# A batched x·yᵀ on Trainium2: five slots of 2 MB become two adjacent pairs and a single, with 4 MB stores and 32 KB reads

## The chip, the cores and the metric

The kernel runs on one NeuronCore of one Trainium2 chip. The metric is the time of one execution on the device in microseconds (us), the median of the runs given. Besides these there is one execution taken by the hardware profiler; its span runs from the first to the last instruction. The engines are called PE (TensorE, matmuls), DVE (VectorE), ACT (ScalarE), POOL (GpSimd) and SP (SyncE, which here does nothing but issue DMAs). Sixteen DMA engines move the data between the main memory and the on-chip memory.

## What is computed

```python
# x: 8 x 12 x 512 x 64 fp32,  y: 8 x 12 x 512 x 64 fp32
np.einsum('bhtc,bhsc->bhts', x, y)      # out: 8 x 12 x 512 x 512 fp32
```

For each of the 96 heads (8 x 12) this is a 512 x 64 matrix times the transpose of another 512 x 64 matrix, and 1 MB of output. Read are 25.17 MB in all, written 100.66 MB.

## The kernel before, in words

**Groups and tiles.** The 96 heads go in 6 groups of 16 (`NG`). A group's x, and its y, is one load of 2 MB into a slot of 128 partitions with 16 KB each: 12 loads, `load(0)` to `load(11)`, x and y in turn. A group has two halves of 8 heads, so there are 12 halves (`NH`). A half gives 8 MB of output in 4 results of 2 MB (`V`), each again 128 partitions with 16 KB. So 48 results `o` are stored, each from one slot.

**Slots.** Five slots of 2 MB (`SLOTS`) serve loads and results alike. `slot()` (L123) gives them out in turn, 0 to 4 and again. A slot's next user waits until the last one has read or stored it; `emit` (L86) keeps for every buffer who wrote and who reads it, and `need` (L71) turns that into waits on semaphores. Each slot has a semaphore of its own for its DMAs.

**From load to product.** `compress(n)` (L136) makes bf16 of a load: for x one ACT copy into `xk`, for y four casts into `yb` (two by DVE, one by POOL, one by ACT). `mix` (L160) rearranges a half's x into `xb` by 32-partition copies, by POOL for the first three halves and by DVE for the rest. `transposes` (L175) turns `xb` and `yb` with DVE into `xT` and `yT`, which are there twice, for halves in turn. `products` (L197) makes 4 matmuls of 128 x 512 into one of the two PSUM buffers `pm`, and a copy (L110; by ACT, and by DVE for the two results in `late`) brings it to half a slot. Two of these make a result.

**Stores.** `store(o, s)` (L211) sends a slot's 2 MB out: 128 reads of 16 KB from the partitions, 128 writes of 16 KB to the output, in an order of 64 x 2 rows. ACT issues every third store and the last four (`by_act`, L208); those wait in `later` until the first copy of the next result is under way (L229). SP issues the others, and all loads.

**The order of the work** is that of the program's lines from L245 on; each engine runs its own instructions in this order. SP first issues five loads. A loop over the 12 loads (L257) then compresses load n and issues load n + 5 for n below 5; load 10 is issued after n = 6 and load 11 after n = 8, into the slots 1 and 3. The four results of the first half come in the same loop: the first after `compress(8)`, the second after `compress(9)`, the third after `compress(10)`, the fourth ahead of `compress(11)`. The other 44 results follow, and after every fourth the transposes and the mixing for a later half (`prepare`, L237).

Of the kernel before, what the change touches and what calls it, by code (L numbers as in the profile page):

```python
# [9 lines left out]
def kernel(  # L10
# [8 lines left out]

    nc = tc.nc
    B, H, T, C = x.shape
    _, _, S, _ = y.shape
    P = 128
    G = 16
    Q = P // G
    R = T // Q
    NG = B * H // G  # L40
    NH = 2 * NG
    V = G // 4
    K = 8
    E = R // K
    D = 32
    SLOTS = 5
    fp32 = mybir.dt.float32
    bf16 = mybir.dt.bfloat16
    u32 = mybir.dt.uint32
    COPY = mybir.ActivationFunctionType.Copy  # L50
    assert C == 2 * D and S == T and R == 2 * D and Q * V == D

    xv = x.rearrange("b h t c -> (b h t c)").rearrange("(g p n) -> g p n", p=P, n=R * C)
    yv = y.rearrange("b h t c -> (b h t c)").rearrange("(g p n) -> g p n", p=P, n=R * C)
    ov = out.rearrange("b h t s -> (b h t s)").rearrange(
        "(o u h q n) -> o h q u n", u=2, h=V, q=Q * E, n=K * S
    )

    sb = ctx.enter_context(tc.tile_pool(name="sb", bufs=1))
    ps = ctx.enter_context(tc.tile_pool(name="ps", bufs=1, space=bass.MemoryType.PSUM))  # L60
    slots = [sb.tile([P, K * S], fp32, name=f"slot{i}") for i in range(SLOTS)]
    xks = [sb.tile([P, R, C], bf16, name=f"xk{i}") for i in range(NG - 1)]
    ybs = [[sb.tile([P, R // 2 * D], u32, name=f"yb{h}{i}") for i in range(NG - 1 + h)] for h in range(2)]
    xbs = [sb.tile([P, K * E * D], u32, name=f"xb{half}") for half in range(2)]
# [2 lines left out]
    pms = [ps.tile([P, 4, S], fp32, name=f"pm{i}") for i in range(2)]  # L67
    engines = {"act": nc.scalar, "dve": nc.vector, "pool": nc.gpsimd, "pe": nc.tensor, "sp": nc.sync}
    sems, ticks, known, snaps, writer, readers = {}, {}, {e: {} for e in engines}, {}, {}, {}

    def need(name, points):  # L71

        best = {}
        for p, v in points:
            if known[name].get(p, 0) < v:
                best[p] = max(best.get(p, 0), v)
        for p, v in list(best.items()):
            if any(snaps[q, w].get(p, 0) >= v for q, w in best.items() if q != p):
                del best[p]
        for p, v in best.items():  # L80
            engines[name].wait_ge(sems[p], v)  # L81
            known[name][p] = v
            for q, w in snaps[p, v].items():
                known[name][q] = max(known[name].get(q, 0), w)

    def emit(name, make, reads=(), writes=(), dma=None):  # L86

        points = [writer[r] for r in (*reads, *writes) if r in writer]
        points += [v for w in writes for v in readers.get(w, ())]
        if name == "pool" and name in ticks:  # L90
            points.append((name, ticks[name]))
        need(name, points)
        p, step = (name, 1) if dma is None else (f"dma{dma}", 16)
        if p not in sems:
            sems[p] = tc.alloc_semaphore(p)
        make().then_inc(sems[p], step)
        at = (p, ticks.get(p, 0) + step)
        ticks[p] = at[1]
        snaps[at] = {**known[name], p: at[1]}
        if dma is None:  # L100
            snaps[at][name] = at[1]
        for r in reads:
            readers.setdefault(r, []).append(at)
        for w in writes:
            writer[w], readers[w] = at, []

    made_slots, loaded, later, late = [], {}, [], (V * NH - V - 1, V * NH - 1)
    in_front = ["dve", "pool", "dve", "act"]

    def copy(name, dst, src, reads, writes):  # L110
        emit(
            name,
            lambda: nc.scalar.activation(dst, src, COPY)  # L113
            if name == "act"
            else engines[name].tensor_copy(dst, src),  # L115
            reads,
            writes,
        )

    def both(i):  # L120
        return [("slot", i, 0), ("slot", i, 1)]

    def slot():  # L123
        made_slots.append(len(made_slots) % SLOTS)
        return made_slots[-1]

    def load(n):
        i = loaded[n] = slot()
        emit(
            "sp",  # L130
            lambda: nc.sync.dma_start(slots[i], (yv if n % 2 else xv)[n // 2]),  # L131
            writes=both(i),
            dma=i,
        )
# [40 lines left out]
    def transposes(i):  # L175
        g, half = divmod(i, 2)
        b = g % (NG - 1 + half)
        emit(
            "dve",
            lambda: nc.vector.transpose(  # L180
                xTs[half].rearrange("p (k r e) -> p k e r", k=K, e=E),
                xbs[half].rearrange("p (k e c) -> p k e c", k=K, e=E),
            ),
            [("xb", half, part) for part in range(4)],
            [("xT", half)],
        )
        emit(
            "dve",
            lambda: nc.vector.transpose(  # L189
                yTs[half].rearrange("p (r j) -> p j r", r=D),  # L190
                ybs[half][b].rearrange("p (j c) -> p j c", c=D),
            ),
            [("yb", half, b, ch) for ch in range(2)],
            [("yT", half)],
        )

    def products(o, k):  # L197
        i, h = divmod(o, V)
        xT = xTs[i % 2].bitcast(bf16).rearrange("p (k h m) -> p k h m", k=K, h=V)
        yT = yTs[i % 2].bitcast(bf16)  # L200
        for j in range(4):
            last = nc.tensor.matmul(  # L202
                pms[k // 4][:, j, :], xT[:, k + j, h, :], yT[:, h * S:(h + 1) * S],
                start=True, stop=True,
            )
        return last

    def by_act(o):  # L208
        return o % 3 == 2 or o >= V * NH - V

    def store(o, s):  # L211
        i, h = divmod(o, V)
        name = "act" if by_act(o) else "sp"
        emit(
            name,
            lambda: engines[name].dma_start(ov[i, h], slots[s]),
            reads=both(s),
            dma=s,
        )

    def result(o, s):

        ot = slots[s].rearrange("p (r s) -> p r s", s=S)
        for k in range(0, K, 4):
            pm = k // 4
            half = o // V % 2
            emit("pe", lambda: products(o, k), [("xT", half), ("yT", half)], [("pm", pm)])
            copy("dve" if o in late else "act", ot[:, k:k + 4, :], pms[pm], [("pm", pm)], [("slot", s, pm)])
            if k == 0:  # L229
                while later:  # L230
                    store(*later.pop())
        if by_act(o):
            later.append((o, s))
        else:
            store(o, s)

    def prepare(i):  # L237

        if i < NH:
            transposes(i)  # L240
        if i + 1 < NH:
            for part in range(4):
                mix(i + 1, "dve", part)

    with tc.tile_critical():  # L245
        load(0)
        for half, name in enumerate(("dve", "pool")):
            emit(
                name,
                lambda: engines[name].memset(xbs[half], 0.0),  # L250
                writes=[("xb", half, part) for part in range(4)],
            )
        need("sp", [("pool", 1)])
        for g in range(1, SLOTS):
            load(g)
        front = []
        for n in range(2 * NG):  # L257
            if n == 11:
                result(3, slot())
            compress(n)  # L260
            mix(n // 4, "pool", n % 4)
            if n == 4:
                transposes(0)
            if n < 5:
                load(n + SLOTS)
            elif n in (6, 8):
                load(n // 2 + 7)
            elif n < 10:
                front.append(slot())
            if n > 7 and n < 11:  # L270
                result(n - 8, front[n - 8])
            if n == 9:
                transposes(1)
        prepare(2)
        for o in range(V, V * NH):
            result(o, slot())
            if o % V == V - 1:
                prepare(o // V + 2)
        store(*later.pop())
        for i, name in enumerate(("dve", "pool", "dve", "pe", "act")):  # L280
            need(name, [(f"dma{i}", ticks[f"dma{i}"])])
# [30 lines left out]
```

## Time and profile before

| what | value |
|---|---|
| median of 3 runs | 300.97 us (300.89 to 301.33) |
| profiled execution, span | 299.1 us (299.07 in the trace) |
| ACT busy | 204.1 us (68%) |
| DVE busy | 160.7 us (54%) |
| PE busy | 129.2 us (43%), mean granted clock 0.796 |
| POOL busy | 56.0 us (19%) |
| SP's DMA queue (q1) | 6048 packets, 88.08 MB, 69.3% of 16 engines |
| ACT's DMA queue (q10) | 2592 packets, 37.75 MB, 29.6% of 16 engines |
| stores, issue to landing | 16.7 us (SP), 14.8 us (ACT), medians |
| copy of half a result by ACT | 1884 ns, 92 of them |

How to read it: the profiled span is 1.9 us shorter than the median of the runs, which also have what lies around it. A busy share is of the whole span. The two queue shares are the time that packets took, summed over the 16 DMA engines and divided by 16 spans. In the tables by line, a group of instructions is given as engine, operation and output tile from input tile; most copies have the line of a helper (L113, L115), so a group is told apart by its tiles. The timeline lists a start, a length, and the instructions that were merged. The chain of waits follows the last instruction back to what released it; in this profile 57% of it is DMA and 22% ACT.

### The profile page before, as it was taken

Reading aid. Unit: us, or ns where it says so; the run is one execution under the profiler, and the core shown is the slowest. Engines: PE = TensorE matmul, PEld = TensorE weight load, DVE = VectorE, ACT = ScalarE, POOL = GpSimd, SP = SyncE. Lnnn points to the kernel's source line nnn. Section 1 sums busy time; section 2 is a strip of 40 time slices with the busy share of each in tenths; the row PEclk is TensorE's granted clock in tenths of the full one; section 3 lists DMA queues with packets and bytes.
Section 4 is the critical chain, followed back from the end, with each engine's and each line's share of the span. In section 5 each row is a group of like instructions: output and inputs, shape, how many; then the busy total and the mean of one; then the engine's idle time right before and its main releaser. Section 6 shows DMA issues by size and latency. Waiting matters only on the chain.

```text
span 299.1 us, 1163 instructions
## 1 busy us (share of the span) xinstructions
PE 129.2 (43%) x377; PEld 35.4 (12%) x384; DVE 160.7 (54%) x77; ACT 204.1 (68%) x105; POOL 56.0 (19%) x23
## 2 busy tenths in 40 slices
PE   0000040547556556474545565554546464567100
PEld 0000010111111111111111111111111111111000
DVE  2167897999839590940946819319276340500500
ACT  1665676999999895687776868685959595549000
POOL 2399999991000000000000000000000000000000
PEclk9999995657799977685979685959795959775655
DMA  7999999999999999999999999999999999999996
GB/s 267 432 427 436 430 425 421 436 432 430 425 438 432 423 436 433 425 430 436 432 423 437 430 421 436 434 427 425 436 430 425 425 427 425 432 425 425 430 425 256
DMA packets 8645, 125.90 MB, mean 421 GB/s; under 512 B 960, under 2 KB 960, under 8 KB 960
## 3 DMA queue, kind: packets, MB, share of 16 engines
q1 hardware_dynamic: 6048, 88.08, 69.3%
q10 hardware_dynamic: 2592, 37.75, 29.6%
q8 instruction: 3, 0.05, 0.1%
q14 instruction: 2, 0.02, 0.0%
HBM read 25.17 MB, written 100.66 MB: 421 GB/s over the span
## 4 chain that ended last, share of the span: by engine, by line
DMA 57%; ACT 22%; PE 6%; issue 5%; DVE 3%; POOL 1%; SPq 0%; ACTq 0%; POOLq 0%
DMA out_dram<-slot 44%; ACT slot L113 19%; DMA slot<-in_y_dram 7%; DMA slot<-in_x_dram 6%; PE pm L202 6%; DVE yb L115 2%; DVE slot L115 2%; ACT xk L113 1%; ACT yb L113 1%; POOL xb L250 1%; SPq L131 0%; ACTq L81 0%; POOLq L307 0%; SPq L245 0%
## 5 line engine op out<-in xcount | busy, mean ns | idle before, releaser
L113 ACT ACTIVATE slot<-pm 128x2048 f32<-128x2048 f32 x92 | 166.6, 1884 | 49.8 <-DMA out_dram<-slot 41.9
L202 PE MATMUL pm<-yT,xT 128*128 128x512 bf16 x377 | 129.2, 482 | 148.3 <-ACT slot L113 108.3
L180 DVE STREAM_TRANSPOSE xT<-xb 128x2048 uint32<-128x2048 uint32 x12 | 46.6, 3887 | 71.3 <-PE pm L202 68.9
L202 PEld LDWEIGHTS pm<-yT,xT 128*128 128x128 bf16 x384 | 35.4, 113 | 241.6 <-ACT slot L113 140.3
L115 DVE COPY xb<-xk 32x2048 bf16<-32x2048 bf16 x36 | 46.9, 1303 | 1.0
L115 DVE CAST yb<-slot 64x2048 bf16<-64x2048 f32 x12 | 36.2, 3013 | 17.0 <-DMA slot<-in_y_dram 16.8
L115 POOL COPY xb<-xk 32x2048 bf16<-32x2048 bf16 x12 | 36.2, 3019 | 10.5 <-ACT xk L113 9.7
L113 ACT ACTIVATE xk<-slot 128x4096 bf16<-128x4096 f32 x6 | 21.7, 3617 | 16.4 <-DMA slot<-in_x_dram 16.4
L115 DVE COPY slot<-pm 128x2048 f32<-128x2048 f32 x4 | 9.0, 2286 | 29.4 <-PE pm L202 29.4
L189 DVE STREAM_TRANSPOSE yT<-yb 128x1024 uint32<-128x1024 uint32 x12 | 23.1, 1921 | 0.0
L113 ACT ACTIVATE yb<-slot 64x2048 bf16<-64x2048 f32 x6 | 14.7, 2457 | 5.1 <-DMA slot<-in_y_dram 5.1
L115 POOL CAST yb<-slot 64x2048 bf16<-64x2048 f32 x6 | 17.8, 2968 | 1.4 <-DMA slot<-in_y_dram 0.8
L250 DVE MEMSET xb<- 128x2048 uint32 x1 | 1.8, 1765 | 1.4 <-SPq L245 1.4
L113 ACT ACT_TABLE_LOAD x1 | 1.3, 1283 | 0.9 <-SPq L245 0.9
L250 POOL MEMSET xb<- 128x2048 uint32 x1 | 1.8, 1804 | 0.5 <-SPq L245 0.5
L296 POOL MEMSET const-float32-0.0<- 128x1 f32 x1 | 0.1, 98 | 0.2 <-issue 0.2
L296 POOL MEMSET const-float32-1.0<- 128x1 f32 x1 | 0.1, 98 | 0.0
L296 POOL MEMSET const-bfloat16-1.0<- 128x1 bf16 x1 | 0.1, 98 | 0.0
L296 POOL MEMSET const-uint8-127<- 128x1 uint8 x1 | 0.1, 98 | 0.0
## 6 DMA issues: line engine op xcount, KB each, us to landing
out_dram<-slot SPq DMA_DIRECT2D x30, 2048.0 KB, 16.7
out_dram<-slot ACTq DMA_DIRECT2D x18, 2048.0 KB, 14.8
slot<-in_x_dram SPq DMA_DIRECT2D x6, 2048.0 KB, 17.3
slot<-in_y_dram SPq DMA_DIRECT2D x6, 2048.0 KB, 20.3
```

What stands on the lines that cost most here:

```text
L113: lambda: nc.scalar.activation(dst, src, COPY)
L115: else engines[name].tensor_copy(dst, src),
L180: lambda: nc.vector.transpose(xTs[half].rearrange("p (k r e) -> p k e r", k=K, e=E), xbs[half].rearrange("p (k e c) -> p k e c", k=K, e=E),),
L189: lambda: nc.vector.transpose(yTs[half].rearrange("p (r j) -> p j r", r=D), ybs[half][b].rearrange("p (j c) -> p j c", c=D),),
L202: last = nc.tensor.matmul(pms[k // 4][:, j, :], xT[:, k + j, h, :], yT[:, h * S:(h + 1) * S], start=True, stop=True,)
L250: lambda: engines[name].memset(xbs[half], 0.0),
L296: nc = _bacc.Bacc("TRN2", target_bir_lowering=False, num_devices=1)
```

## The change

Slots 0 and 1 become one buffer of 128 partitions with 32 KB each, slots 2 and 3 another, and slot 4 stays by itself. They lie at fixed places; the rest of the memory is given out as before.

- **Stores.** Two results in an adjacent pair of slots go out in one DMA of 4 MB: 128 reads of 32 KB, and 256 writes of 16 KB in an order of 64 x 4 rows. Such a pair is made of the results 0 and 2, or 1 and 3, of a half, since these lie at one step in the output. Other results go out by themselves as before. A table (`plan`) says which result goes where: in the first half a pair and two singles, in the second a single, a pair and a single, and then in turn two pairs, or a single, a pair and a single. That makes 17 stores of 4 MB and 14 of 2 MB.
- **Loads.** Loads 2 to 11 read 64 rows of 32 KB and write 128 rows of 16 KB. Loads 0 and 1 stay as they were.
- **How they are issued.** `wide` makes the DMA instruction by hand, with the two sides' access patterns as they are given.
- **Who issues.** SP issues all stores but those of the last half, which ACT issues. DVE makes the copies of one result, the last, instead of two.
- **Order.** Load 10 is issued after `compress(7)` into slot 2, and load 11 after `compress(8)` into slot 3. In the first half the results are made in the order 0, 2, 1, 3; the first store comes after result 2.

```diff
-    slots = [sb.tile([P, K * S], fp32, name=f"slot{i}") for i in range(SLOTS)]
+    xw, yw = (a.rearrange("(g p n) -> g p n", p=P // 2, n=2 * N) for a in (xf, yf))
+    ow = of.rearrange("(o a j q n) -> o j q a n", a=4, j=2, q=Q * E, n=N)
+    pairs = [nc.alloc_sbuf_tensor(f"slots{i}", [P, 2 * N], fp32)[:, :] for i in range(2)]
+    slots = [p[:, j * N:(j + 1) * N] for p in pairs for j in range(2)]
+    slots.append(nc.alloc_sbuf_tensor("slot", [P, N], fp32)[:, :])
...
+    places = [0, 1, 2, 3, 4, 0, 1, 2, 3, 4, 2, 3]
+    steady = [
+        [(0, 2, 0), (1, 3, 2)],
+        [(0, 4), (1, 3, 0), (2, 4)],
+        [(0, 2, 2), (1, 3, 0)],
+        [(0, 4), (1, 3, 2), (2, 4)],
+    ]
+    plan = [[(0, 2, 0), (1, 4), (3, 2)], [(0, 3), (1, 3, 0), (2, 4)]]
+    plan += [steady[i % 4] for i in range(2, NH)]
...
+    def place(ap, dims):
+        name = ap.tensor.name
+        pattern = [ap.ap[0], *[[1, 1]] * (dims - len(ap.ap)), *ap.ap[1:]]
+        return mybir.PhysicalAccessPattern(
+            ap=pattern, offset=ap.offset, dtype=ap.dtype, memref=name, memsetref=f"{name}_set"
+        )
+
+    def wide(name, dst, src):
+        return engines[name].add_instruction(
+            mybir.InstDMACopy(
+                name=nc.get_next_instruction_name(),
+                engine=engines[name].engine,
+                ins=[place(src, len(dst.ap))],
+                outs=[place(dst, len(dst.ap))],
+                mode="Copy",
+                cce_op=mybir.AluOpType.bypass,
+                queue="qActDynamicHW" if name == "act" else "qSPDynamicHW",
+            )
+        )
+
     def load(n):
-        i = loaded[n] = slot()
+        i = loaded[n] = places[n]
         emit(
             "sp",
-            lambda: nc.sync.dma_start(slots[i], (yv if n % 2 else xv)[n // 2]),
+            lambda: nc.sync.dma_start(slots[i], (yv if n % 2 else xv)[n // 2])
+            if n < 2
+            else wide("sp", slots[i], (yw if n % 2 else xw)[n // 2]),
...
-    def store(o, s):
-        i, h = divmod(o, V)
-        name = "act" if by_act(o) else "sp"
+    def store(i, *what):
+        *hs, s = what
+        name = "act" if i == NH - 1 else "sp"
         emit(
             name,
-            lambda: engines[name].dma_start(ov[i, h], slots[s]),
-            reads=both(s),
+            lambda: wide(name, ow[i, hs[0]], pairs[s // 2])
+            if len(hs) == 2
+            else engines[name].dma_start(ov[i, hs[0]], slots[s]),
+            reads=both(*range(s, s + len(hs))),
             dma=s,
         )
...
+    def results(i, *what):
+        *hs, s = what
+        for j, h in enumerate(hs):
+            result(i, h, s + j)
+        if i == NH - 1:
+            later.append((i, *what))
+        else:
+            store(i, *what)
...
             if n < 5:
                 load(n + SLOTS)
-            elif n in (6, 8):
-                load(n // 2 + 7)
-            elif n < 10:
-                front.append(slot())
-            if n > 7 and n < 11:
-                result(n - 8, front[n - 8])
-            if n == 9:
+            elif n in (7, 8):
+                load(n + 3)
+            if n == 8:
+                result(0, 0, 0)
+            elif n == 9:
+                result(0, 2, 1)
+                store(0, *plan[0][0])
                 transposes(1)
+            elif n == 10:
+                results(0, *plan[0][1])
         prepare(2)
-        for o in range(V, V * NH):
-            result(o, slot())
-            if o % V == V - 1:
-                prepare(o // V + 2)
+        for i in range(1, NH):
+            for what in plan[i]:
+                results(i, *what)
+            prepare(i + 2)
         store(*later.pop())
```

More of the change, by code (lines that the diff above doesn't have):

```diff
@@ L46 @@
     SLOTS = 5
+    N = K * S
     fp32 = mybir.dt.float32
@@ L50 @@
     COPY = mybir.ActivationFunctionType.Copy
[L51 to L57, printed above, removed]
+    assert C == 2 * D and S == T and R == 2 * D and Q * V == D and N == R * C
+    xf, yf, of = (a.rearrange("b h t c -> (b h t c)") for a in (x, y, out))
+    xv, yv = (a.rearrange("(g p n) -> g p n", p=P, n=N) for a in (xf, yf))
+    xw, yw = (a.rearrange("(g p n) -> g p n", p=P // 2, n=2 * N) for a in (xf, yf))
+    ov = of.rearrange("(o u h q n) -> o h q u n", u=2, h=V, q=Q * E, n=N)
+    ow = of.rearrange("(o a j q n) -> o j q a n", a=4, j=2, q=Q * E, n=N)
+    pairs = [nc.alloc_sbuf_tensor(f"slots{i}", [P, 2 * N], fp32)[:, :] for i in range(2)]
+    slots = [p[:, j * N:(j + 1) * N] for p in pairs for j in range(2)]
+    slots.append(nc.alloc_sbuf_tensor("slot", [P, N], fp32)[:, :])
     sb = ctx.enter_context(tc.tile_pool(name="sb", bufs=1))
     ps = ctx.enter_context(tc.tile_pool(name="ps", bufs=1, space=bass.MemoryType.PSUM))
-    slots = [sb.tile([P, K * S], fp32, name=f"slot{i}") for i in range(SLOTS)]
     xks = [sb.tile([P, R, C], bf16, name=f"xk{i}") for i in range(NG - 1)]
@@ L105, in emit @@
             writer[w], readers[w] = at, []
-    made_slots, loaded, later, late = [], {}, [], (V * NH - V - 1, V * NH - 1)
+    loaded, later = {}, []
     in_front = ["dve", "pool", "dve", "act"]
+    places = [0, 1, 2, 3, 4, 0, 1, 2, 3, 4, 2, 3]
[7 more added lines that the diff above has]
+    plan += [steady[i % 4] for i in range(2, NH)]
     def copy(name, dst, src, reads, writes):
@@ L118, in copy, with both @@
         )
[L120 to L125, printed above, removed]
+    def both(*ids):
+        return [("slot", i, pm) for i in ids for pm in range(2)]
+    def place(ap, dims):
[16 more added lines that the diff above has]
+        )
     def load(n):
-        i = loaded[n] = slot()
+        i = loaded[n] = places[n]
         emit(
             "sp",
-            lambda: nc.sync.dma_start(slots[i], (yv if n % 2 else xv)[n // 2]),
+            lambda: nc.sync.dma_start(slots[i], (yv if n % 2 else xv)[n // 2])
+            if n < 2
+            else wide("sp", slots[i], (yw if n % 2 else xw)[n // 2]),
             writes=both(i),
@@ L206, in products, with result @@
         return last
-    def by_act(o):
-        return o % 3 == 2 or o >= V * NH - V
-    def store(o, s):
-        i, h = divmod(o, V)
-        name = "act" if by_act(o) else "sp"
+    def store(i, *what):
+        *hs, s = what
+        name = "act" if i == NH - 1 else "sp"
         emit(
             name,
-            lambda: engines[name].dma_start(ov[i, h], slots[s]),
-            reads=both(s),
+            lambda: wide(name, ow[i, hs[0]], pairs[s // 2])
+            if len(hs) == 2
+            else engines[name].dma_start(ov[i, hs[0]], slots[s]),
+            reads=both(*range(s, s + len(hs))),
             dma=s,
         )
-    def result(o, s):
+    def result(i, h, s):
         ot = slots[s].rearrange("p (r s) -> p r s", s=S)
+        late = i == NH - 1 and h == plan[i][-1][-2]
         for k in range(0, K, 4):
             pm = k // 4
-            half = o // V % 2
-            emit("pe", lambda: products(o, k), [("xT", half), ("yT", half)], [("pm", pm)])
-            copy("dve" if o in late else "act", ot[:, k:k + 4, :], pms[pm], [("pm", pm)], [("slot", s, pm)])
+            half = i % 2
+            emit("pe", lambda: products(i * V + h, k), [("xT", half), ("yT", half)], [("pm", pm)])
+            copy("dve" if late else "act", ot[:, k:k + 4, :], pms[pm], [("pm", pm)], [("slot", s, pm)])
             if k == 0:
@@ L231, in result @@
                     store(*later.pop())
-        if by_act(o):
-            later.append((o, s))
+    def results(i, *what):
[4 more added lines that the diff above has]
+            later.append((i, *what))
         else:
-            store(o, s)
+            store(i, *what)
     def prepare(i):
@@ L253 @@
         need("sp", [("pool", 1)])
-        for g in range(1, SLOTS):
-            load(g)
-        front = []
+        for n in range(1, SLOTS):
+            load(n)
         for n in range(2 * NG):
             if n == 11:
-                result(3, slot())
+                results(0, *plan[0][2])
             compress(n)
```

## The prediction

> **What bounds the kernel now.** I read the page from its second part, the span in forty slices, and the packet line under it.
>
> ```profile
> DMA  7999999999999999999999999999999999999996
> GB/s 267 432 427 436 430 425 421 436 432 430 425 438 432 423 436 433 425 430 436 432 423 437 430 421 436 434 427 425 436 430 425 425 427 425 432 425 425 430 425 256
> DMA packets 8645, 125.90 MB, mean 421 GB/s; under 512 B 960, under 2 KB 960, under 8 KB 960
> ```
>
> The 16 DMA engines are full from the second slice to the last but one. The trace's packet records say the same to the nanosecond: from the first packet at 1.99 us to the last data at 297.6 us no engine idles, through loads and stores alike. So the span is 1.99 us of start, 480 packets of 16 KB on each engine, and about 1.5 us of end. Only two things can move it: what a packet takes, and a hole in the stream. Both the load stage and the store stage run at nearly one rate, as the windows by stage show (the last two columns are the DMA's busy share and GB/s):
>
> ```profile
> 10.00:30.00 20.00, 0.00 (x0) 0.00 (x0) 11.21 (x4) 12.55 (x5) 17.06 (x6) 1.00 1.00 429
> 60.00:100.00 40.00, 22.93 (x74) 6.35 (x73) 31.37 (x16) 39.50 (x22) 8.40 (x3) 0.83 1.01 431
> 200.00:290.00 90.00, 43.39 (x128) 11.84 (x128) 36.12 (x18) 53.48 (x30) 0.00 (x0) 0.77 1.01 428
> ```
>
> ACT (the fourth engine in these rows) is busy 39.50 of 40 us between 60 and 100 us. There ACT is as full as the DMA, so what it makes later, the DMA gets later. The timelines of ACT, DVE and SP around the first stores are what the holes are worked out from:
>
> ```profile
> 57.60 3.65 ACT L113 ACTIVATE slot<-pm 128x2048 f32<-128x2048 f32 x2
> 61.27 3.62 ACT L113 ACTIVATE xk<-slot 128x4096 bf16<-128x4096 f32 x1
> 64.80 3.63 ACT L113 ACTIVATE slot<-pm 128x2048 f32<-128x2048 f32 x2
> ...
> 83.97 10.73 ACT L113 ACTIVATE slot<-pm 128x2048 f32<-128x2048 f32 x6
> ```
> ```profile
> 36.75 13.71 DVE L115 CAST yb<-slot 64x2048 bf16<-64x2048 f32 x4
> ```
> ```profile
> 41.80 0.33 SPq L131 DMA_DIRECT2D slot<-in_x_dram  x1
> 51.59 0.33 SPq L131 DMA_DIRECT2D slot<-in_y_dram  x1
> 55.12 6.69 SPq L216 DMA_DIRECT2D out_dram<-slot  x2
> ```
>
> Here the first result is stored at 55.12 and the second at 61.27, while by the packet records the twelfth load keeps the engines until 61.53 (first engine) to 62.13 (last). The early store at 55.12 is the cover that the change takes away.
>
> **Part 1: the packets.** In the records of 10 to 30 us a 16 KB packet starts every 607 ns on its engine, and a transfer's 4-byte closing packet takes 6 ns: 8 x 607 + 6 = 4862 ns per 2 MB, seen again and again. Two rows price a packet apart from its data: the 4-byte packet's 6 ns, and two undisturbed 8 KB records of 309 ns beside 611 ns for 16 KB (2 x 309 - 611 = 7). I take 5 ns a packet, so about 602 ns of data. The change makes 32 KB reads; writes stay 16 KB, so the trace of before can't say whether the 5 ns belong to a read or to a write. Bounds: nothing (they belong to the write) and 7 ns per read saved. Below nothing: a read could lose by being paired with two writes; the nearest row is that loads of 128 rows and stores of 64 x 2 rows both run at 4862 ns, so unequal sides have cost nothing here, and I leave 2 ns for it. I take 5, the nearest row to a bare packet. [...]
>
> There are 17 pair stores and 14 single ones in place of 48. A pair saves 8 reads x 5 + one closing packet of 6 = 46 ns per engine. A wide load saves 4 x 5 = 20 ns: loads 2 to 8 together 0.14 us, which is how much sooner load 8 lands. ACT runs without slack from that landing (47.95) on, so all its times below move up by 0.14.
>
> **Part 2: the holes in front.** (a) Load 10 now goes into slot 2, which DVE's casts of load 7 read; they end at 36.75 + 13.71 = 50.46, where before the issue stood at 41.80. Load 11 behind it on SP waits for ACT anyway until 51.56. How long from an issue to the first packet with an empty queue? One row: the first load, issued at 0.96, first packet at 1.99, 1.03 us, of which 0.39 is the issue. Store issues take 0.54 to 0.65, so I take 1.2 us for stores; bounds 1.03 and 1.7 (an issue of 4 MB twice as long). Load 10 then starts at 51.5 to 51.7, and the engines are through with load 9 at 51.57: a hole of 0 to 0.1 us, swallowed by the next. (b) The first pair needs the second result: issue 61.27 - 0.14, first packet 62.33 instead of 61.53: 0.8 us late. (c) Three singles follow (issues about 68.4, 72.3 and 78.5, all earlier than needed) and end at 62.33 + 9.68 + 3 x 4.86 = 86.59. The second pair is made by ACT's 74.81 to 85.88 row of tiles: issue 85.88 - 0.14, first packet 86.94. In before the transfer in this place started at 85.86. So from here the stream is **1.08 us late** (0.9 with 1.03, 1.6 with 1.7). A restart could cost more: the first load's packets took 0.96 us over the usual; at (b) 0.35 of that is hidden by (c), so I leave up to 0.6 for it.
>
> [...]
>
> **Part 3: the steady stage.** Slots now come free two at a time. The tightest place is in each odd half: single slot 4 is stored, a pair, slot 4 again, then a pair. From the landing of the first single the DMA has 9.7 + 4.9 = 14.6 us of queued work, while ACT must fill a tile and a pair (6 copies of 1.9 = 11.4), plus 0.4 from last data to landing and 1.2 to the first packet: 13.0. It fits with 1.6 us to spare; the other places have 3.7 or more. So no hole, and ACT, PE and DVE stay hidden. SP now has ACT's stores too: 31 issues in 299 us, each behind ACT's copies in the order in which these end, so nothing earlier waits behind one. In the last half ACT's first store stands behind a copy that waits for a pair to land; one pair (9.7 us) is queued meanwhile. The last store waits for slot 4 with a pair queued. Both cost nothing while that cover stands.
>
> **Sum.** From the second pair on, 16 pairs x 46 ns = 0.74 us gained. 299.07 + 1.08 - 0.74 = 299.4 us of span. The median of the runs is 300.97, 1.9 above the profiled span, and I add the same difference: 300.97 + 0.34 = **301.3 us**, 0.1% slower. About 0.2% (0.6 us) is what a measurement of this kernel can tell from no change.
>
> **Rivals.**
> 1. *The writes hold the 5 ns* (slower). Both sides' packets must pass, and 16 KB writes remain. Then only 16 x 6 ns = 0.1 us comes back, ACT isn't early, and the start is 85.88 + 1.2 - 85.86 = 1.22 late: **302.1 us**. For it: loads and stores have one pitch, so nothing shows the read side to be the slow one. It decides when a pair saves less than 30 ns ((1.08 - 0.6) / 16). The same time comes if the descriptors are cut back to 16 KB after all (the change doesn't do what it says); the instruction built by hand, without the usual load call, speaks against that.
> 2. *A wide read also hides small stalls* (faster). The mean pitch from 86 to 286 us is 4886 ns per tile, not 4862. If a pair ran at its data alone (16 x 602 + 6, 4819 per tile), 32 tiles x 67 ns = 2.1 us against 1.08: **300.0 us**. For it: the records of 611 grow to 614 to 618 after 200 us; against: these stalls hit loads of 30 to 60 us as well, where nothing tells reads from writes.
> 3. *Holes return in each odd half* (slower). If the way from a pair's last data to its landing takes 2.1 us more than I count, the 1.6 us are gone and 5 places lose 0.5 each: 301.3 + 2.5 = **303.8 us**. For it: engines drift by 1 to 3 us, and a pair waits for the slowest; against: the slowest sets the end and has the cover in full.
>
> **How the numbers follow.** Forecast 0.40 (own range 300.7 to 301.9, from 0.9 to 1.6 of lateness), rival 1 0.28 (0.05 of it the cut descriptors), rival 2 0.22, rival 3 0.10. Of the forecast about 0.27 lies within 0.2%, 0.07 above and 0.06 below; of rival 2 0.18 is faster, 0.04 within. So faster 0.24, same 0.31, slower 0.45. The range: low end 299.8, rival 2 with nearly all it asks; high end 302.9, rival 1 with 0.6 us of restart and a little over; that leaves out rival 3 and the edge of rival 2.
>
> **What would show it.** Records of 32 KB at under 1214 ns a piece mean part 1 is right; 1214 or two of 607 mean rival 1. The DMA row should have a dent at 62 us and a smaller one near 86, SP's pair issues at about 61.1 and 85.7, and then none; a dent every 39 us means rival 3. The forecast falls if the dent at 62 is missing, if it lasts over 2 us, or if single stores' pitch changes too.

## The result, and the profile after

The changed kernel takes **302.53 us** (median of 5 runs, 302.12 to 302.83), against 300.97 before (5 runs, 300.82 to 301.33): a ratio of 1.0048, 95% interval 1.0037 to 1.0059, so 1.56 us slower. The profiled execution's span is 300.78 us in place of 299.07. The forecast was 301.3; the time is inside the stated range (299.8 to 302.9), outside the forecast case's own one (300.7 to 301.9).

The page of the changed kernel, its second part and the packet line:

```profile
DMA  7999999999999999999999999999999999999995
GB/s 277 438 449 436 418 423 418 397 436 386 421 453 416 421 416 479 423 415 427 418 418 436 466 416 418 415 423 444 421 442 431 394 455 416 418 453 440 427 407 233
DMA packets 5557, 125.90 MB, mean 419 GB/s; under 512 B 688, under 2 KB 688, under 8 KB 688
```

The busy digits show nothing: the DMA engines stand at 9 from the second slice to the last but one, as before, and the kernel is slower. What moved is in the packets. There are 3088 fewer, since 2816 records now have 32 KB, and the rate sags to 397 and 386 in the slices at 52 and 67 us. The rates of single slices jump because a record counts where it starts; the windows are steadier. Again the last two columns are the DMA's share and GB/s:

```profile
10.00:30.00 20.00, 0.00 (x0) 0.00 (x0) 11.22 (x4) 12.56 (x5) 17.05 (x6) 1.00 1.03 443
60.00:100.00 40.00, 23.03 (x74) 6.29 (x74) 29.73 (x16) 38.39 (x21) 9.55 (x3) 0.88 0.99 424
200.00:290.00 90.00, 40.44 (x130) 11.24 (x132) 31.58 (x16) 57.52 (x33) 0.00 (x0) 0.80 1.00 429
```

From 60 to 100 us it was 431 and is 424: the loss is in front. SP's timeline and ACT's in that place:

```profile
50.51 0.47 SPq L134 DMA_DIRECT2D slots<-in_x_dram  x1
51.58 0.47 SPq L134 DMA_DIRECT2D slots<-in_y_dram  x1
61.27 0.63 SPq L134 DMA_DIRECT2D out_dram<-slots  x1
68.44 0.56 SPq L236 DMA_DIRECT2D out_dram<-slot  x1
...
85.98 0.54 SPq L134 DMA_DIRECT2D out_dram<-slots  x1
```
```profile
74.91 3.65 ACT L115 ACTIVATE slots<-pm 128x2048 f32<-128x2048 f32 x2
78.77 7.18 ACT L115 ACTIVATE slots<-pm 128x2048 f32<-128x2048 f32 x4 [0.21 <-PE pm L223]
```

Load 10 is issued at 50.51, the first pair at 61.27 and the second at 85.98, right as ACT ends its four copies. To place the loss I used the trace's packet records and asked when each 2 MB of the stream starts:

| the stream's n-th 2 MB starts at, us | before | after | later by |
|---|---|---|---|
| 10th | 46.85 | 46.71 | -0.14 |
| 12th (load 11) | 56.64 | 57.52 | 0.88 |
| 13th (first pair) | 61.53 | 62.56 | 1.03 |
| 18th (second pair) | 85.86 | 87.18 | 1.32 |
| 31st | 149.17 | 150.77 | 1.60 |
| 60th, the last | 291.08 | 292.58 | 1.50 |

So 1.32 us are lost up to the second pair. Little of it is idle time: by the records the engines idle for 0.12 us each at 52, 0.09 at 62 and 0.10 at 87 us, and the first reads of load 10 alone lose 0.9. (These starts differ by 0.1 to 0.4 us between executions from the first loads on, so a single lateness is good to about that.) In the 42 steps from there to the last the stream should have won back most of 0.74 us, by the prediction; it lost 0.18 more (4.890 us a step in place of 4.886). Two questions follow: what sets the 1.32, and where did the gain go.

### The profile page after: what moved, and what is told of

Read it like the earlier page. It is cut to its first block, busy times and chain, and to the rows that moved or that the text cites. A ratio compares the mean times of both kernels' runs of the same rounds, so it can differ in the third digit from the quotient of the medians.

```text
span 300.8 us, 1130 instructions
## 1 busy us (share of the span) xinstructions
PE 123.1 (41%) x377; PEld 34.0 (11%) x384; DVE 154.4 (51%) x75; ACT 206.8 (69%) x107; POOL 57.2 (19%) x23
## 4 chain that ended last, share of the span: by engine, by line
DMA 50%; ACT 33%; PE 5%; issue 4%; DVE 3%; POOL 1%; SPq 0%; ACTq 0%; POOLq 0%; DVEq 0%
DMA out_dram<-slot 28%; ACT slots L115 23%; DMA out_dram<-slots 8%; ACT slot L115 7%; DMA slots<-in_y_dram 7%; DMA slots<-in_x_dram 6%; PE pm L223 5%; DVE yb L117 2%; DVE slot L117 1%; ACT yb L115 1%; ACT xk L115 1%; POOL xb L276 1%; SPq L134 0%; SPq L150 0%; ACTq L73 0%
## 5 line engine op out<-in xcount | busy, mean ns | idle before, releaser
L115 ACT ACTIVATE slots<-pm 128x2048 f32<-128x2048 f32 x72 | 129.8, 1895 | 20.7 <-DMA out_dram<-slots 17.8
L115 ACT ACTIVATE slot<-pm 128x2048 f32<-128x2048 f32 x22 | 40.6, 1913 | 28.2 <-DMA out_dram<-slot 28.1
L117 DVE CAST yb<-slots 64x2048 bf16<-64x2048 f32 x10 | 29.6, 2961 | 14.8 <-DMA slots<-in_y_dram 14.6
L115 ACT ACTIVATE xk<-slots 128x4096 bf16<-128x4096 f32 x5 | 18.1, 3617 | 13.9 <-DMA slots<-in_x_dram 13.9
L117 POOL CAST yb<-slots 64x2048 bf16<-64x2048 f32 x5 | 15.4, 3089 | 2.1 <-DMA slots<-in_y_dram 1.7
L115 ACT ACTIVATE yb<-slots 64x2048 bf16<-64x2048 f32 x5 | 12.3, 2465 | 5.1 <-DMA slots<-in_y_dram 5.1
L117 DVE CAST yb<-slot 64x2048 bf16<-64x2048 f32 x2 | 4.7, 2366 | 2.4 <-DMA slot<-in_y_dram 2.4
L115 ACT ACTIVATE xk<-slot 128x4096 bf16<-128x4096 f32 x1 | 3.6, 3617 | 2.5 <-DMA slot<-in_x_dram 2.5
L117 POOL CAST yb<-slot 64x2048 bf16<-64x2048 f32 x1 | 3.5, 3510 | 0.1
L115 ACT ACTIVATE yb<-slot 64x2048 bf16<-64x2048 f32 x1 | 2.5, 2462 | 0.0
```

## The experiments

All times are medians of runs, compared with the kernel before on the same chip (300.88 to 301.0 us).

**e1, what sets the lateness in front: the second pair's issue, or the late load 10.** After its late issue load 10's first reads took 1.7 to 2.3 us per 32 KB in place of 1.22, 0.9 us lost on each engine, a large part of the whole.

```diff
-    places = [0, 1, 2, 3, 4, 0, 1, 2, 3, 4, 2, 3]
+    places = [0, 1, 2, 3, 4, 0, 1, 2, 3, 4, 1, 0]
...
-    plan = [[(0, 2, 0), (1, 4), (3, 2)], [(0, 3), (1, 3, 0), (2, 4)]]
-    plan += [steady[i % 4] for i in range(2, NH)]
+    plan = [[(0, 2, 2), (1, 4), (3, 1)], [(0, 0), (1, 3, 2), (2, 4)]]
+    plan += [steady[(i - 2) % 4] for i in range(2, NH)]
...
-            elif n in (7, 8):
-                load(n + 3)
+            elif n in (6, 8):
+                load(n // 2 + 7)
...
```

> The changed kernel with the two pairs of slots exchanged, so that load 10 goes into slot 1 and is issued after compress(6), near 41.8 us as before the change, instead of 50.5; everything else in the same order. Theory A (the second pair's issue at about 86.0 sets the lateness in front): the 18th transfer still starts near 87.2, the time stays within 0.3 us of the changed kernel's 302.5, and a hole of about 0.8 us shows up at 62 us instead of the slow first reads at 52. Theory B (the 0.9 us that load 10's first reads lose at 52 us after the queue ran dry are what the change costs): the time falls by 0.9 to 1.1, to about 301.5.

Measured: 302.72 us, ratio 1.0057 (1.0045 to 1.0070), not told apart from the changed kernel. SP's timeline of e1:

```profile
41.76 0.47 SPq L134 DMA_DIRECT2D slots<-in_x_dram  x1
43.59 0.47 SPq L134 DMA_DIRECT2D slots<-in_y_dram  x1
61.23 0.64 SPq L134 DMA_DIRECT2D out_dram<-slots  x1
...
85.95 0.54 SPq L134 DMA_DIRECT2D out_dram<-slots  x1
```

Load 10 goes out at 41.76 and its slow reads are gone; in their place the engines stand idle for 0.96 us each between 60 and 65 us. The 18th step starts at 87.15, as in the changed kernel. Theory A holds, and B falls: the delay that a later, larger one covers cost nothing that could be told (302.72 us against 302.53). (Near 87 us the engines idle for only 0.12 us here: by then the first pair's hole has made the stream nearly as late as the second pair's issue does. e7 and e10 part the two.)

**e2, the front in singles.** The eight results of the first two halves go out one by one, as before the change.

```diff
...
+    plan = [[(0, 0), (1, 2), (2, 4), (3, 0)], [(0, 1), (1, 2), (2, 3), (3, 4)]]
+    plan += [steady[(i - 2) % 4] for i in range(2, NH)]
...
+            if n > 7 and n < 11:
+                results(0, *plan[0][n - 8])
...
```

> The changed kernel with the front as it was before the change: the eight results of the first two halves go out by themselves as soon as they are made, load 10 goes early into slot 1 and load 11 into slot 3; pairs begin with the third half. Theory A: the 18th transfer starts near 85.9 as before the change, 1.3 us earlier, and the time is 301.2 (301.0 to 301.5). Two pairs fewer cost 0.1. Theory B says the same here, 301.4 to 301.6. If the lateness lies in the steady stage instead, nothing changes: 302.4.

Measured: **300.45 us, ratio 0.9981 (0.9972 to 0.9989): faster than both kernels**, by 0.5 and 2.1 us. That is 0.75 under what theory A gave, so more than 1.3 us of lateness had gone. The 18th step starts at 85.81, and the rest of the stream is quicker as well, 4.868 us a step in place of 4.890, with the same wide stores. Its window from 90 to 160 us, and that of the changed kernel below it:

```profile
90.00:160.00 70.00, 36.50 (x122) 10.20 (x120) 40.28 (x25) 52.89 (x30) 0.00 (x0) 0.85 1.01 432
```
```profile
90.00:160.00 70.00, 37.89 (x117) 10.31 (x117) 40.27 (x24) 53.25 (x30) 0.00 (x0) 0.80 1.00 427
```

432 GB/s against 427, a stage in which neither has a hole over 0.1 us. In the records the 32 KB pieces take 1213 ns nearly all through here (mean 1214), in the changed kernel 1221. Something in front slows what comes long after it.

**e3, the changed kernel with 16 KB reads in its stores.**

```diff
-            lambda: wide(name, ow[i, hs[0]], pairs[s // 2])
+            lambda: engines[name].dma_start(ow[i, hs[0]], pairs[s // 2])
```

> The changed kernel with the pair stores issued by the usual call, 4 MB as before but each read cut to 16 KB. Theory C (a wide read saves 5 ns a piece, and its own small stalls give this back): records of 611 ns, without the 9 ns of stall that the wide ones have on average; the pitch of 2 MB from 90 to 200 us is 4862 to 4870 ns and the time is within 0.3 us of 302.5. Theory D (the stalls come from the order of the writes or the single queue, and wide reads do gain): the stalls stay, the pitch goes to 4910 to 4930 ns and the time to 303.3 or more.

Measured: 303.85 us, ratio 1.0092 (1.0076 to 1.0107), 1.3 us over the changed kernel. Records of 16 KB have a mean of 617 ns from 90 to 160 us. The stalls stay without wide reads, and the time rises: theory C falls, and wide reads do gain. (The front is 0.3 us later here than in the changed kernel, at the 18th step; the rest comes behind it.)

**e4, the kernel before with one queue for its stores.**

```diff
-        return o % 3 == 2 or o >= V * NH - V
+        return o >= V * NH - V
```

> The kernel before the change with all stores but the last four issued by SP, nothing else. Theory C: no change, 300.97 within 0.3, and the records of 60 to 200 us stay at 611. Rival D1 (two queues keep the engines' stream smooth and one does not): records rise to 615 or more in 60 to 200 us and the time by 0.6 to 1.0.

Measured: 300.94 us, ratio 1.0003 (0.9994 to 1.0011), records at 611 (mean 611.5). Here it makes no difference who issues the stores.

**e6 and e8, what the wide reads are worth in stores and in loads**, in e2, where nothing else disturbs. e6 has e3's edit, and e8 issues all loads as before the change (`if n < 12` for `if n < 2`).

> Run e2 (single results in front, pairs of 4 MB from the third half on), with each read of a pair store cut to 16 KB. What is left out against e2 is only the widening of the stores' reads. If the read is worth 5 ns a piece: 15 pairs x 8 x 5 = 0.6 us, 301.0 to 301.1, and clean records of 611. If the write holds the cost and e2's gain comes from 4 MB stores or from SP's queue: 300.45 as e2.

> Run e2 with all loads as before the change, 16 KB on both sides. By the records of e2 the wide loads ran at 4882 ns per 2 MB, as the plain ones in e4 do, their small stalls taking what the fewer reads saved: no change, 300.45 within 0.2. If the saving in loads holds: 0.2 slower, 300.65.

Measured: e6 301.42 us (ratio 1.0013, 1.0004 to 1.0022), e8 300.55 (0.9983, 0.9974 to 0.9992). In the stores the widening is worth 0.97 us, more than the 0.6 expected; without it pairs are a little slower than singles. About 0.3 us of the difference is there by the 37th step (178 us), as the count gives; the rest comes behind it, where the records of e6 have means of 614 to 618 in stretches of 10 us. In the loads it isn't told from nothing (0.10 us). In their records nothing is won from 20 to 60 us: the wide ones mostly take 1222 to 1227, as much as two of 611 to 615.

**e7, the second half's pair alone.** e2 with `[(0, 1), (1, 3, 2), (2, 4)]` as its second half.

> Run e2 with the second half as in the changed kernel: a single, a pair and a single. Only the hole in front of this pair, issued at about 85.8, remains; the first half goes out in singles. Theory A (the second pair's issue sets the lateness): the 18th transfer starts near 87.0 in place of 85.8, one hole of 1.1 to 1.3 us, and with theory E stalls after it: 302.0 to 302.5. If the first pair's hole is what counts: 300.5 to 300.9.

Measured: 302.42 us, ratio 1.0047 (1.0035 to 1.0060): one pair, put one half too early, costs nearly all that the change costs, 1.97 us of 2.08 against e2. SP's row of it:

```profile
85.91 0.54 SPq L134 DMA_DIRECT2D out_dram<-slots  x1
```

The engines are idle for 1.1 us each, and the 18th step starts at 87.11, 1.30 late against e2; the last step starts 2.02 late, so 0.72 us is lost behind the hole. Records of 16 KB have a mean of 611.4 from 68 to 86 us, ahead of the hole, and 617 from 90 to 160, behind it.

**e5 and e9, one hole in the kernel before**, to see whether a hole slows a stream that has no pair and no wide read. In e5 the first store only moved in the program, behind the making of the second result; SP still found it ready at 55.14, so there was no hole, and e5 says only that this leaves the time alone (301.03 us, 1.0002, 0.9994 to 1.0011). e9 makes it wait for the second result.

```diff
-            reads=both(s),
+            reads=both(s) + (both(2) if o == 0 else []),
...
+        elif o == 0:
+            held.append((o, s))
         else:
+            while held:
+                store(*held.pop())
             store(o, s)
```

> The kernel before the change with one thing altered: the first result's store is issued only when the second result is made, at about 61.2 us instead of 55.1, so that the stream has one hole of 0.8 to 0.9 us at 62 and none later. All reads are 16 KB, all stores 2 MB. Theory E (after a hole the 16 engines start in step, and their packets then disturb each other): records of 70 to 160 us rise from 611 to 614 or more, and the time by the hole and 0.5 to 0.8 more, to 302.3 to 302.7. Rival (a hole costs its length; the stalls belong to wide reads or to the pairs): the records stay at 611, 301.8 to 302.0.

> Run e5 mended: in e5 the store only moved in SP's program and still went out at 55.1, so that it had no hole. Here the first result's store waits for the second result's copies as well, near 61.3, and the second store follows it. One hole of about 0.8 us at 62 in the kernel before, all else as it was, reads of 16 KB. Theory E (after a hole the engines run in step and disturb each other): records of 70 to 160 us rise from 611 to 614 or more, a pitch of 4880 to 4900 ns, and 302.3 to 302.7. Rival (a hole costs its length only): 301.8 to 302.0, records at 611.

Measured: e9 303.14 us, ratio 1.0079 (1.0066 to 1.0093). The timeline of SP and the windows in e9, then the second window in the kernel before:

```profile
51.47 0.33 SPq L131 DMA_DIRECT2D slot<-in_y_dram  x1
61.15 28.70 SPq L216 DMA_DIRECT2D out_dram<-slot  x6
```
```profile
50.00:62.00 12.00, 5.86 (x14) 1.51 (x15) 9.56 (x5) 11.93 (x7) 11.74 (x4) 0.91 0.96 407
90.00:160.00 70.00, 37.36 (x116) 10.22 (x116) 40.04 (x24) 52.96 (x30) 0.00 (x0) 0.80 1.01 427
```
```profile
90.00:160.00 70.00, 39.45 (x121) 10.68 (x120) 40.40 (x25) 55.02 (x31) 0.00 (x0) 0.83 1.01 431
```

The engines are idle for 0.8 us each at 62 us and never again. The stream is 0.92 us late there (62.45 for 61.53), and then goes at 4.911 us a step in place of 4.886, with records of 617 ns in place of 611.5 at once after the hole and of 616 to the end. The whole cost is 2.2 us: more than half of it comes after the hole. That a hole slows what follows is thus shown; how is asked below. But the loss doesn't grow to the end: against the kernel before, the stream is 1.16 us late at the 18th step, 1.93 at the 37th (180 us), 2.23 at the 49th (239 us) and 2.22 at the last. From 210 us on the records of the kernel before have means of 615 to 616 too, without a hole.

**e10, the first pair alone** (e1 with singles in the second half), to see what its hole costs by itself.

> Run e1 with the second half in four singles, so that of the two holes in front only that of the first pair (issued at 61.2) is left. The 18th transfer should start 0.9 late, near 86.7. Theory E: then 300.45 + 0.9 for the hole + 0.6 to 0.8 for the stalls behind it, 301.9 to 302.2. Rival (length only): 301.3 to 301.5.

Measured: 302.17 us, ratio 1.0043 (1.0031 to 1.0056). The 18th step starts at 86.83, and the stalls are there from 68 us on (616.6 ns). A hole like e9's (0.65 us idle here, 0.8 there), and 0.97 us less. Over the last 42 steps e10 takes 0.92 us less than e9, where e2 takes 0.74 less than the kernel before: wide stores are worth no less behind a hole.

**e11 and e12, is it the step?** In the records of e9 at 80 us, the 16 packets in flight had all started within 143 ns of each other, taken modulo a packet (607 ns); at the same time it is 331 ns in the kernel before and 494 in e2. So behind e9's hole the engines start nearly together, in step. e11 is e9 with small loads of few rows that put some engines behind others after the hole; e12 is its control, with small loads of 16 rows for all engines alike.

```diff
...
+                for j, (rows, cols) in enumerate(((8, 960), (8, 960), (4, 960), (2, 480), (1, 240))):
+                    emit("sp", lambda: nc.sync.dma_start(pad[16 * j:16 * j + rows, :cols], xv[0][:rows, :cols]), dma=5 + j)
...
```

> Run e9 (the kernel before with one hole at 62 us) with five small loads into an unused tile right behind the first store, of 8, 8, 4, 2 and 1 rows, so that they fall on fewer than 16 engines and put these behind the others by up to about 0.5 us; SP issues the second store some 2 us later, while the first still runs. The hole stays. Theory E with the engines' common step as the cause: the 16 engines' packets start at different times again, the records fall back to 611 up to 160 us, and the time is 0.8 to 1.2 under e9, 302.0 to 302.4. Rival (something else that a hole leaves, not the step): 303.1 to 303.7, records at 614 or more.

> The same with five small loads of 16 rows, which give every engine the same small extra work: the control to e11, with nearly the same bytes and as many issues, and no engine put behind another. Both theories: as e9, 303.1 to 303.5, records at 614 or more. If it falls like e11, it is the small loads themselves and not their uneven spread.

Measured: e11 303.43 us (ratio 1.0079, 1.0066 to 1.0093), e12 303.88 (1.0096, 1.0082 to 1.0110). The forecast of 302.0 to 302.4 is missed. SP's rows behind the hole, of e11 and then of e12:

```profile
61.37 0.65 SPq L217 DMA_DIRECT2D out_dram<-slot  x1
62.07 4.28 SPq L243 DMA_DIRECT2D pad<-in_x_dram  x5
66.39 24.02 SPq L217 DMA_DIRECT2D out_dram<-slot  x5
```
```profile
61.19 0.64 SPq L217 DMA_DIRECT2D out_dram<-slot  x1
61.87 5.00 SPq L243 DMA_DIRECT2D pad<-in_x_dram  x5
66.92 22.97 SPq L217 DMA_DIRECT2D out_dram<-slot  x5
```

That e11 is 0.45 us under its control is not the work of the spread. The second store of e12 went out half a microsecond later, and the engines stood idle a second time, for 0.27 us at 68. From the 18th step to the last, e9, e11 and e12 need the same 206.3 us.

The spread itself did come, though as two groups some 300 ns apart and not as sixteen places. The starts lie within 364 ns from 72 to 86 us and within 442 ns from 120 to 160 (medians), in the kernel before within 428 from 90 to 160. Yet the records of e11 only go to 615.0 (68 to 86 us) and 615.7 (90 to 160), not to 611. So the step, in this measure, is not what keeps the records long. A finer order of the engines, or something else that a hole leaves, may be; this stays open.

The mean length of records, without the few over 1.2 times, sorts the runs, up to 160 us, by one thing, whether a hole came ahead. How long the engines idled doesn't set it alone: in the changed kernel it is about 0.1 us at each of the three places, with the slow first reads at 52.

| mean of 16 KB / 32 KB records, ns | 68 to 86 us | 90 to 160 us |
|---|---|---|
| before, e4 | 611.5 / - | 611.5 / - |
| e6 | 611.5 / - | 611.5 / - |
| e2 | 611.4 / - | 611.5 / 1214 |
| e7 (hole at 86) | 611.4 / - | 617 / 1221 |
| after (holes at 52, 62, 86) | 615.8 / 1222 | 617 / 1221 |
| e10 (hole at 62) | 616.6 / 1224 | 617 / 1221 |
| e9 (hole at 62) | 617 / - | 616 / - |

From 200 to 285 us all of them, with a hole or without, have 16 KB records of 615 to 616 ns.

## Why the prediction was right or wrong

**Bound.** Right: the DMA stream is full (its share is 0.98 to 1.03 in the windows from 10 to 290 us), and only what packets take and idle time moved the time.

**Part 1, the packets.** Right for stores, and rival 1 is out. Clean wide records are 1213 ns against two of 611, one start per 1209 against 1214: 5 ns a read, as taken. From the 18th step to the last e2 takes 0.74 us less than the kernel before, where 15 pairs x 46 ns give 0.69. e6 minus e2 puts the widening at 0.97 us for 15 pairs (0.6 by count), and e3 finds a gain again. Wrong for loads: their 0.14 us by load 8 did not come (it landed at 47.91, before at 47.92), so ACT was not early. The table's -0.14 is not that gain: the 10th 2 MB starts as early in e4 (46.72), whose loads are as before.

**Part 2, the holes.** The mechanism is right and was read off ACT's and SP's rows: the second pair's issue sets when its transfer starts, as e1 and e7 show (alone, the first pair makes the 18th step start at 86.83, the second at 87.11). The terms: 1.2 us from issue to first packet was taken and 1.20 measured (85.98 to 87.18); the lateness was 1.08 and measured 1.32, the difference being ACT's missing 0.14 and 0.1 us of ACT's own. What load 10 lost was rightly called covered, but it was 0.9 us, taken at 0 to 0.1, and mostly slow reads and not idle time; so the dent at 62 us, forecast at 0.8, was 0.09 us idle. Of the 1.20 us, 0.54 is the issue itself and 0.66 the rest. The low end of the forecast's own range, 300.7, doesn't follow from the 0.9 us of lateness named for it, which gives 301.1; 0.5 us would give it, and no run shows that for the second pair: 1.32 was measured, and 1.30 in e7.

**Part 3, the steady stage.** Right: the only idle times behind the front are of 0.19 us near 219 us and of 0.04 near 181. Rival 3 did not happen. SP's 31 issues are a miscount (28 stores and 12 loads; ACT issues 3 stores), on which nothing hung.

**The sum is the step that failed.** It read "From the second pair on, 16 pairs x 46 ns = 0.74 us gained", and so took the stream behind a hole to run at the pace of an undisturbed one. It doesn't. By e9 a hole adds 25 ns a step (4.911 against 4.886), 42 x 0.025 = 1.05 us; the wide stores take off 21 (4.890 against 4.911), 0.88 us. So 1.32 + 1.05 - 0.88 = 1.49, where the last step starts 1.50 late. These terms add up by how they are formed, since the changed kernel's own pace is one of them. What shows the effect without it is e7 against e2: wide stores in both, one hole, and 0.72 us lost behind it.

The gain was there and was more than paid back. Part 2 left 0.6 us for a restart, as a cost on the spot; it is spread over the stream instead, up to some 240 us (e9: 0.92 us late at the hole, 2.23 at 239 us), and nothing in the trace of before had a hole to show it. Two of the prediction's own signs against its forecast came: the dent at 62 us all but missing, and the single stores' records changed too (611.5 to 617 ns). Its sign for rival 1, 32 KB records of 1214 ns or more, also came (1221), but from the stalls, since it is 1214 in e2 and below that in most of its records.

That the time lies inside the stated range is in part luck: the upper end came from rival 1 and a restart cost on the spot, and neither is what the time went to. Rival 1's 302.1 came near the time for a wrong reason. Rival 2's 300.0 was nearly met in e2 alone, by a kernel without the holes, and not by its mechanism: a pair's pieces start every 1209 ns there, not every 1204.

## What to carry to other kernels

On a stream that is full, look first for the place where the work before it has no slack, and leave the transfers there small and early: pairs from the third half on won 0.5 us (e2), and with two more of them put in front the kernel lost 1.6. Price a hole in a full DMA stream at more than its length, here 2.2 us for 0.9, and check the records behind it, since the busy share doesn't show it (1.01 from 90 to 160 us in e9 and in the kernel before alike). A wider read was worth 5 ns per 32 KB in stores here (a start every 1209 ns against 1214), and in loads nothing that could be told (0.10 us, e8).

## What the runs showed of the hardware that was not expected

- After an idle time of 0.65 to 1.1 us on all 16 DMA engines, 16 KB store packets took 616 to 617 ns in place of 611.5 for the next 70 us and more (e7, e9, e10). In the changed kernel, 0.1 us idle and slow first reads went ahead of the same (615.8 and 617).
- A load issued as the queue ran empty had first reads of 1.7 to 2.3 us for 32 KB (after, at 52 us; in e3 the window from 50 to 62 us is as here, a share of 0.99 and 393 GB/s). The pair stores that restart the stream at 62.56 and 87.18 us in the changed kernel have first reads of 1.21 to 1.22 us, and over the five steps behind e9's restart at 62 us no more than 0.24 us was lost (0.92 to 1.16 late).
- Stalls that look alike come without a hole: in the kernel before, records have a mean of 615 in the loads from 30 to 60 us, and again from 200 us on. Its three 16 KB packets of the instruction queue (q8) came at 107, 178 and 254 us and took 0.96 us each. Whether they bring the stalls was not tried; behind those at 107 and 178 the means stay at 611 to 613 for 20 us and more.
